# Idle products before the first load, other banks for the last down projection, and a re-ordered last normalisation in a two-layer encoder

## The chip, the cores and the metric

One core of a Trainium2 chip runs the whole program. Its engines work side by side, each on its own instruction queue: TensorE (PE; its weight loads are listed as PEld), VectorE (DVE), ScalarE (ACT), GpSimd (POOL) and SyncE (SP), which here only issues transfers. The metric is the time of one execution on the device in microseconds (us).

## The reference, cut to what matters

The reference is a two-layer encoder on 512 tokens of width 1024, all in float32. Each layer is a mixing sublayer (dilated attention, gated MLP and pooling between one input and one output projection) and a mixture of experts, each followed by a normalisation of `alpha * x + h`:

```python
def reference(x, ...):
    for l in range(DEPTH):
        h = _mixing_sublayer(x, w_in[l], w_out[l], ...)
        x = _layernorm(DEEPNORM_ALPHA * x + h, ln1_g[l], ln1_b[l])
        h = _moe(x, router_w, router_bias, w_gate[l], w_up[l], w_down[l])
        x = _layernorm(DEEPNORM_ALPHA * x + h, ln2_g[l], ln2_b[l])
    return x
```

`_moe` routes each token to two of 16 experts. An expert computes `(silu(x Wg) * (x Wu)) Wd`, with an inner width of 512; the two results are added with their gates. `_layernorm` subtracts the row's mean, divides by the root of its variance plus 1e-5, multiplies by `g` and adds `b`.

## The kernel before, in words

**Products.** Each float32 matrix is split into a high and a low part (ACT copies the high part in a rounded format, DVE subtracts it: `hilo`, L211 to L213, and for weights `emit_hi` and `emit_lo`, L184 and L192). `mm3` (L215) then issues three products per 128 x 512 block: high by high, high by low, low by high.

**Weights.** They come in blocks of 1 MB. A block is two halves; each half is split by ACT and DVE some steps ahead of its use. `half` (L203) first emits the splits up to four halves ahead (`splits_to`, L196), then hands over the half that is due. High and low parts live in a ring of four buffers each. So DVE's queue holds the splits of later halves between the other work, in the order in which the program emits them.

**The order of the work.** Every engine issues its instructions in the order of the program's text. Waits between engines follow from the data and from the reuse of buffers; a buffer or bank is free once all that touch its old content have run.

**The start.** SP fetches the activations (`xr`) and the first weights in slices. For each slice ACT and DVE make the parts, and PE starts the first projection of layer 0: four steps of 24 products, each step on one half of the weights and two slices of the activations. `load_consts` (L101) fetches constants and fills `one16`, a 128 x 128 block of 16-bit ones that the routing uses later, on POOL. The banks of PE's results come from three pools: four in `bankA`, two in `bankY`, two in `bankT`.

**An expert.** `up_piece` (L908) makes gate and up product in two `bankA` banks, `act` (L919) the activation, `turn_h` its transpose, `down_piece` (L936) the down product in two `bankY` banks, and `finish_y` (L955) scales by the gate out of the banks. Step `e` of the loop does the up product of expert `e` and the down product of expert `e - 1`. The down product goes half by half and in each half bank by bank; only for the last expert of layer 1 it goes bank by bank over all four halves, both banks in the call with `n == 0`. Experts 0 to 13 add their rows in device memory. The last two (`LAST`) are kept on the core, each as a high and a low part: `finish_y` has ACT write `y[0]` and DVE `y[1]` from each bank (L965, L966). For expert 15 these are the buffers `gl` and `y`; the pool of `y` has two buffers.

**The end of a layer.** The rows so far are fetched into four tiles `xs[0]` to `xs[3]` of 128 tokens. `add_last(i)` (L1089) forms, for each half `j` of a tile, four products on PE, which place the rows of experts 14 and 15, in a `bankT` bank, and adds the bank to `xs[i]`. What follows hangs on the tile's letter in `MODE` (L71):

- "F" and "C": DVE adds the bank (L1105); DVE takes mean and variance by the batch-norm instructions (`ln_stats`), POOL makes the factor in two small steps (L222, L223). "F" then normalises in two DVE passes over the tile (`ln_apply`, L244 and L245); "C" uses ACT and POOL too.
- "P": PE adds `xs[i]` itself by a product with the identity (L1097), ACT copies bank to tile and sums (L1103); DVE makes the mean (L1109), ACT squares the centred tile into a `y` buffer that nobody reads and sums (L1111), POOL makes the factor (L1112, L1113), and `norm` makes two DVE passes (L1128, L1129).

In layer 1 (`l + 1 == L`) `prep(i + 1)`, `norm(i)` and the store of tile `i` by SP (L1138) alternate. In layer 0 the tiles are normalised in between transposes and the first products of layer 1.

Of the kernel before, what the change touches and what calls it, by code (L numbers as in the profile page):

```python
# [59 lines left out]
def encoder(ctx, tc, a, out):  # L60
# [10 lines left out]
    MODE = ("FPCC", "FFPP")  # L71
# [29 lines left out]
    def load_consts():  # L101
        nc.sync.dma_start(cb, a["consts"])
        nc.sync.dma_start(rw, a["router_w"])
        nc.sync.dma_start(rb, a["router_b"])
        G.memset(one16, 1.0)
        G.memset(mhalf, -0.5)
# [172 lines left out]
    def layer(l, xst, xh, xl, tail):  # L279
# [656 lines left out]
        def down_piece(e, n):  # L936
            if n == 0:
                ES[e]["y"] = (bankY(), bankY())
            hh, hl = ES[e]["hT"]
            if e == NE - 1 and l + 1 == L:  # L940
                if n == 0:
                    w = [half(("e", l, e, 4 + k // 2), k % 2, NS - k) for k in range(4)]
                    for j in range(2):
                        ws = slice(j * 512, (j + 1) * 512)
                        for k in range(4):
                            mm3(ES[e]["y"][j][0:CAP], hh[:, k], hl[:, k], w[k][0][:, ws], w[k][1][:, ws], k == 0, k == 3)
# [142 lines left out]
        def add_last(i):  # L1089
            sums = None  # L1090
            if MODE[l][i] == "P":
                sums = sp.tile([128, 4], F32, name="sums", bufs=3)
            for j in range(2):
                js = slice(j * 512, (j + 1) * 512)
                b = bankT()
                if sums is not None:
                    T.matmul(b, ident, xs[i][:, js], start=True, stop=False)  # L1097
                for e in LAST:
                    lhs = ES[e]["qT"][:, i * 128:(i + 1) * 128]
                    T.matmul(b, lhs, ES[e]["yl"][0][:, js], start=sums is None and e == LAST[0], stop=False)  # L1100
                    T.matmul(b, lhs, ES[e]["yl"][1][:, js], start=False, stop=e == LAST[1])
                if sums is not None:
                    A.activation(xs[i][:, js], b, AF.Copy, accum_out=sums[:, j:j + 1])  # L1103
                else:
                    V.tensor_tensor(xs[i][:, js], xs[i][:, js], b, op=OP.add)  # L1105
# [9 lines left out]

        stats = {}
# [7 lines left out]

        def norm(i):
            if MODE[l][i] == "P":
                x, t = xs[i], stats[i][1]
                V.scalar_tensor_tensor(x, x, t[:, 2:3], gb2[0], op0=OP.add, op1=OP.mult)  # L1128
# [177 lines left out]
```

## Time and profile before

| | us |
|---|---|
| median of three runs | 1105.14 (1104.51 to 1105.29) |
| the profiled execution | 1104.96 |
| its span, from first to last instruction | 1103.3 |
| PE busy | 1055.1 |
| DVE busy | 883.8 |
| ACT busy | 740.2 |
| POOL busy | 413.7 |

The profile is of one execution. Busy times of different engines overlap. An engine's idle time matters only if the chain of work that ended last runs through it. Lengths of PE's products are modelled: products in a row overlap, and the distance of their starts tells what each takes. A number in brackets behind a row is the engine's idle time ahead of it, with the instruction that ended it.

### The profile page before, as it was taken

How to read it: one execution, taken by the hardware profiler on the slowest of the kernel's cores; microseconds unless marked ns; L12 is line 12 of the kernel's file. 1: busy time of each engine (PE TensorE's matmuls, PEld its weight loads, DVE VectorE, ACT ScalarE, POOL GpSimd, SP SyncE). 2: the span in 40 equal slices, each digit the busy share in tenths (PEclk: the TensorE clock that was granted, in tenths of full speed). 3: DMA queues.
4: the chain of work that ended last, by engine and by line, in shares of the span. 5: the costliest groups of instructions: out<-in, count | busy, mean ns of one | idle time of the engine just before them, and what ended most of it. 6: DMA issues, size and time to landing. Idle time of an engine off the chain costs nothing.

```text
span 1103.3 us, 14619 instructions
## 1 busy us (share of the span) xinstructions
PE 1055.1 (96%) x5160; PEld 817.1 (74%) x5160; DVE 883.8 (80%) x1279; ACT 740.2 (67%) x1020; POOL 413.7 (37%) x325
## 2 busy tenths in 40 slices
PE   7999999999999999999899999899899999999995
PEld 5887776777777777777578877777777777777773
DVE  4433898879999999999756249878899999999996
ACT  4334877248888888888542358862578888888872
POOL 0294554232343525230125836433224343334102
PEclk9999999999999999999899999999999999999998
DMA  8162113979999999995313422249799999999831
GB/s 292 65 229 79 68 57 128 399 272 361 351 369 357 373 350 350 361 352 178 114 45 119 150 77 77 77 154 397 280 336 369 357 354 350 364 360 366 285 122 77
DMA packets 46943, 270.90 MB, mean 246 GB/s; under 512 B 8223, under 2 KB 8479, under 8 KB 19216
## 3 DMA queue, kind: packets, MB, share of 16 engines
q1 hardware_dynamic: 37152, 246.17, 59.4%
q0 software_dynamic: 8704, 19.75, 6.8%
q10 hardware_dynamic: 1008, 3.99, 1.0%
q8 instruction: 42, 0.69, 0.2%
q14 instruction: 37, 0.30, 0.1%
HBM read 257.62 MB, written 23.46 MB: 255 GB/s over the span
## 4 chain that ended last, share of the span: by engine, by line
PE 80%; ACT 8%; DVE 8%; issue 2%; DMA 1%; POOL 0%; SPq 0%; POOLq 0%; ACTq 0%; DVEq 0%
PE bA L218 17%; PE bA L216 17%; PE bA L217 17%; PE bY L216 6%; PE bY L217 6%; PE bY L218 6%; PE bT L263 3%; ACT pr L378 2%; ACT ph L212 1%; PE bA L779 1%; DVE pl L213 1%; DVE pr L371 1%; PE bY L689 1%; DVE kl L354 1%; ACT kh L353 1%
## 5 line engine op out<-in xcount | busy, mean ns | idle before, releaser
L192 DVE TENSOR_TENSOR wlo<-raw,whi 128x1024 fp32r<-128x1024 f32 x277 | 328.8, 1224 | 93.4 <-ACT whi L184 90.5
L184 ACT ACTIVATE whi<-raw 128x1024 fp32r<-128x1024 f32 x283 | 295.7, 1060 | 102.6 <-PE bA L218 67.9
L853 POOL DMA_INDIRECT xs<-x1d,si x26 | 129.1, 4964 | 279.2 <-DVE sg L848 243.7
L216 PE MATMUL bA<-whi,gh 128*112 128x512 f32 x512 | 204.4, 399 | 3.8 <-ACT gh L212 2.7
L218 PE MATMUL bA<-whi,gl 128*112 128x512 f32 x512 | 201.7, 394 | 0.2
L217 PE MATMUL bA<-wlo,gh 128*112 128x512 f32 x512 | 200.7, 392 | 0.0
L216 PE MATMUL bA<-whi,xh 128*128 128x512 f32 x256 | 104.4, 408 | 8.3 <-ACT whi L212 7.8
L216 PEld LDWEIGHTS bA<-whi,gh 128*112 128x112 f32 x512 | 89.1, 174 | 31.4 <-ACT gh L212 3.1
L218 PEld LDWEIGHTS bA<-whi,gl 128*112 128x112 f32 x512 | 89.2, 174 | 31.0 <-DVE gl L213 1.9
L217 PEld LDWEIGHTS bA<-wlo,gh 128*112 128x112 f32 x512 | 89.1, 174 | 27.1
L218 PE MATMUL bA<-whi,xl 128*128 128x512 f32 x256 | 102.5, 400 | 0.0
L217 PE MATMUL bA<-wlo,xh 128*128 128x512 f32 x256 | 102.3, 400 | 0.0
L387 POOL TENSOR_SCALAR pr<-pr,nm 128x512 f32<-128x512 f32 x42 | 67.6, 1617 | 90.8 <-DVE nm L385 75.5
L216 PE MATMUL bY<-whi,hh 128*112 128x512 f32 x240 | 96.5, 402 | 0.0
L218 PE MATMUL bY<-whi,hl 128*112 128x512 f32 x240 | 94.5, 394 | 0.0
L217 PE MATMUL bY<-wlo,hh 128*112 128x512 f32 x240 | 94.3, 393 | 0.0
L858 POOL DMA_INDIRECT accd<-y,si x28 | 56.1, 2004 | 68.8 <-ACT y L971 61.5
L216 PEld LDWEIGHTS bA<-whi,xh 128*128 128x128 f32 x256 | 48.9, 191 | 21.2 <-ACT whi L212 8.6
L192 DVE TENSOR_TENSOR wlo<-qkt,whi 128x1024 fp32r<-128x1024 f32 x48 | 57.1, 1220 | 3.4 <-ACT whi L184 3.4
L192 DVE TENSOR_TENSOR wlo<-pr,whi 128x1024 fp32r<-128x1024 f32 x48 | 57.3, 1220 | 1.4 <-ACT whi L184 1.3
L217 PEld LDWEIGHTS bA<-wlo,xh 128*128 128x128 f32 x256 | 48.8, 191 | 12.8 <-DVE wlo L213 0.9
L218 PEld LDWEIGHTS bA<-whi,xl 128*128 128x128 f32 x256 | 48.6, 190 | 12.4 <-DVE xl L213 0.9
(249 smaller groups left out, 2085.6 us busy)
## 6 DMA issues: line engine op xcount, KB each, us to landing
raw<-w_exp SPq DMA_DIRECT2D x116, 1024.0 KB, 11.9
raw<-w_mix SPq DMA_DIRECT2D x24, 1024.0 KB, 4.8
qkt<-w_exp SPq DMA_DIRECT2D x24, 1024.0 KB, 11.6
pr<-w_exp SPq DMA_DIRECT2D x24, 1024.0 KB, 11.0
er<-w_exp SPq DMA_DIRECT2D x12, 1024.0 KB, 8.0
px<-w_exp SPq DMA_DIRECT2D x12, 1024.0 KB, 10.9
x1d<-xs POOLq DMA_DIRECT2D x8, 512.0 KB, 8.3
accd<-xs SPq DMA_DIRECT2D x8, 512.0 KB, 10.0
```

The lines of the kernel that those rows point to most:

```text
L184: A.activation(hi, raw, AF.Copy)
L192: (eng or V).tensor_tensor(lo, raw, hi, op=OP.subtract)
L212: A.activation(hi, src, AF.Copy)
L213: V.tensor_tensor(lo, src, hi, op=OP.subtract)
L216: T.matmul(ps, xh, wh, start=start, stop=False)
L217: T.matmul(ps, xh, wl, start=False, stop=False)
L218: T.matmul(ps, xl, wh, start=False, stop=stop)
L263: T.transpose(t[:, c * CAP:(c + 1) * CAP], src[0:CAP, (4 * j + c) * 128:(4 * j + c + 1) * 128], ident[0:CAP, 0:CAP])
L378: A.activation(pr[:, i, :], pr[:, i, :], AF.Exp, bias=nm[:, 0, i:i + 1], scale=-1.0, accum_out=nm[:, 1, i:i + 1])
L387: E.tensor_scalar(pr[:, i, :], pr[:, i, :], nm[:, 2, i:i + 1], None, op0=OP.mult)
L853: G.indirect_dma_start(out=dst[0:CAP], out_offset=None, in_=xd[l][:, :], in_offset=bass.IndirectOffsetOnAxis(ap=idx, axis=0), bounds_check ...
L858: G.indirect_dma_start(out=accd[l][:, :], out_offset=bass.IndirectOffsetOnAxis(ap=idx, axis=0), in_=src[0:CAP], in_offset=None, bounds_che ...
```

## The change

It has four parts. Ahead of the first transfers' use, PE gets 48 products of `one16` with itself, 128 columns each, in a `bankT` bank that nobody reads; `one16` is filled by DVE at the top of the program instead of by POOL. The down product of expert 15, in both layers, takes its two banks from `bankA`. In layer 1 its work is cut into two calls, one for each bank, in the same order. In layer 1 the letters of the tiles become "AAPP": a new mode "A", in which DVE's add also sums (no batch-norm statistics) and the mean, the square and the factor go as in "P". The end of layer 1 is written out anew: the halves of tiles 0 and 1 in turns, two in `bankT` and two in `bankY` banks; then the adds of tiles 2 and 3, with the centring passes of tiles 0 and 1 behind the first and their scaling passes and stores behind the second; then centring, scaling and store of tiles 2 and 3. For layer 0 `add_last` and `norm` do what they did.

```diff
--- before.py
+++ after.py
@@ -68,7 +68,7 @@
     NRAW, NS, NRAWX, NQ = 2, 4, 6, 4
     LEAD, VLAG, NLAG = 6, 2, 2
     LAST = (NE - 2, NE - 1)
-    MODE = ("FPCC", "FFPP")
+    MODE = ("FPCC", "AAPP")
     cp = pool(ctx, "cp")
     rawp = pool(ctx, "rawp", NRAW)
     splp = pool(ctx, "splp", NS)
@@ -102,7 +102,6 @@
         nc.sync.dma_start(cb, a["consts"])
         nc.sync.dma_start(rw, a["router_w"])
         nc.sync.dma_start(rb, a["router_b"])
-        G.memset(one16, 1.0)
         G.memset(mhalf, -0.5)
 
     xd = [dr.tile([S, D], F32, name=f"x1d{l}") for l in range(L)]
@@ -935,15 +934,16 @@
 
         def down_piece(e, n):
             if n == 0:
-                ES[e]["y"] = (bankY(), bankY())
+                bank = bankA if e == LAST[1] else bankY
+                ES[e]["y"] = (bank(), bank())
             hh, hl = ES[e]["hT"]
             if e == NE - 1 and l + 1 == L:
                 if n == 0:
-                    w = [half(("e", l, e, 4 + k // 2), k % 2, NS - k) for k in range(4)]
-                    for j in range(2):
-                        ws = slice(j * 512, (j + 1) * 512)
-                        for k in range(4):
-                            mm3(ES[e]["y"][j][0:CAP], hh[:, k], hl[:, k], w[k][0][:, ws], w[k][1][:, ws], k == 0, k == 3)
+                    ES[e]["w"] = [half(("e", l, e, 4 + k // 2), k % 2, NS - k) for k in range(4)]
+                w = ES[e]["w"]
+                ws = slice(n * 512, (n + 1) * 512)
+                for k in range(4):
+                    mm3(ES[e]["y"][n][0:CAP], hh[:, k], hl[:, k], w[k][0][:, ws], w[k][1][:, ws], k == 0, k == 3)
                 return
             for k in range(2):
                 kk = 2 * n + k
@@ -1086,23 +1086,28 @@
                         load_ln(l, "ln2", gb2)
 
 
-        def add_last(i):
-            sums = None
-            if MODE[l][i] == "P":
-                sums = sp.tile([128, 4], F32, name="sums", bufs=3)
-            for j in range(2):
-                js = slice(j * 512, (j + 1) * 512)
-                b = bankT()
-                if sums is not None:
-                    T.matmul(b, ident, xs[i][:, js], start=True, stop=False)
-                for e in LAST:
-                    lhs = ES[e]["qT"][:, i * 128:(i + 1) * 128]
-                    T.matmul(b, lhs, ES[e]["yl"][0][:, js], start=sums is None and e == LAST[0], stop=False)
-                    T.matmul(b, lhs, ES[e]["yl"][1][:, js], start=False, stop=e == LAST[1])
-                if sums is not None:
-                    A.activation(xs[i][:, js], b, AF.Copy, accum_out=sums[:, j:j + 1])
-                else:
-                    V.tensor_tensor(xs[i][:, js], xs[i][:, js], b, op=OP.add)
+        def add_half(i, j, sums, bank=bankT):
+            js = slice(j * 512, (j + 1) * 512)
+            b = bank()
+            keep = MODE[l][i] == "P"
+            if keep:
+                T.matmul(b, ident, xs[i][:, js], start=True, stop=False)
+            for e in LAST:
+                lhs = ES[e]["qT"][:, i * 128:(i + 1) * 128]
+                T.matmul(b, lhs, ES[e]["yl"][0][:, js], start=not keep and e == LAST[0], stop=False)
+                T.matmul(b, lhs, ES[e]["yl"][1][:, js], start=False, stop=e == LAST[1])
+            if keep:
+                A.activation(xs[i][:, js], b, AF.Copy, accum_out=sums[:, j:j + 1])
+            elif sums is not None:
+                V.scalar_tensor_tensor(xs[i][:, js], xs[i][:, js], 1.0, b, op0=OP.mult, op1=OP.add,
+                                       accum_out=sums[:, j:j + 1])
+            else:
+                V.tensor_tensor(xs[i][:, js], xs[i][:, js], b, op=OP.add)
+
+        def new_sums(i):
+            return sp.tile([128, 4], F32, name="sums", bufs=3) if MODE[l][i] in "PA" else None
+
+        def spread(i, sums):
             if sums is None:
                 return ln_stats(xs[i], sp, EPS2)
             t = sp.tile([128, 3], F32, name="lnt", bufs=3)
@@ -1113,6 +1118,12 @@
             G.tensor_tensor(t[:, 1:2], t[:, 0:1], mhalf[:, 0:1], op=OP.pow)
             return None, t
 
+        def add_last(i):
+            sums = new_sums(i)
+            for j in range(2):
+                add_half(i, j, sums)
+            return spread(i, sums)
+
         stats = {}
 
         def prep(i):
@@ -1122,23 +1133,50 @@
             if MODE[l][i] == "C":
                 ln_center(xs[i], stats[i])
 
+        def center(i):
+            V.scalar_tensor_tensor(xs[i], xs[i], stats[i][1][:, 2:3], gb2[0], op0=OP.add, op1=OP.mult)
+
+        def scale(i):
+            V.scalar_tensor_tensor(xs[i], xs[i], stats[i][1][:, 1:2], gb2[1], op0=OP.mult, op1=OP.add)
+
         def norm(i):
-            if MODE[l][i] == "P":
-                x, t = xs[i], stats[i][1]
-                V.scalar_tensor_tensor(x, x, t[:, 2:3], gb2[0], op0=OP.add, op1=OP.mult)
-                V.scalar_tensor_tensor(x, x, t[:, 1:2], gb2[1], op0=OP.mult, op1=OP.add)
+            if MODE[l][i] in "PA":
+                center(i)
+                scale(i)
             else:
                 ln_apply(xs[i], gb2, stats[i], MODE[l][i] == "F")
 
-        prep(0)
         if l + 1 == L:
-            for i in range(NT):
-                prep(i + 1)
-                norm(i)
+            sums = [new_sums(i) for i in range(2)]
+            for j in range(2):
+                for i in range(2):
+                    add_half(i, j, sums[i], (bankT, bankY)[j])
+            for i in range(2):
+                stats[i] = spread(i, sums[i])
+
+            def sent(i):
+                scale(i)
                 nc.sync.dma_start(out[i * 128:(i + 1) * 128, :], xs[i])
+
+            for i in range(2):
+                n = i + 2
+                sums.append(new_sums(n))
+                for j in range(2):
+                    add_half(n, j, sums[n], (bankT, bankY)[i])
+                if i == 0:
+                    center(0)
+                    center(1)
+                else:
+                    sent(0)
+                    sent(1)
+                stats[n] = spread(n, sums[n])
+            for i in range(2, NT):
+                center(i)
+                sent(i)
             ost.close()
             lst.close()
             return None
+        prep(0)
         splits_to(stream["use"] + NS)
         norm(0)
         prep(1)
@@ -1182,13 +1220,17 @@
     with ExitStack() as ist:
         ip = pool(ist, "ip", 1, side="right")
         xr = ip.tile([128, NK, S], F32, name="xr")
+        heat = bankT()
         warm = ip.tile([128, 1], F32, name="warm")
+        V.memset(one16, 1.0)
         V.memset(warm, 0.0)
         A.activation(warm, warm, AF.Copy)
 
         def first(k, n=1):
             nc.sync.dma_start(xr[:, k:k + n], a["xT"][:, k:k + n])
 
+        for _ in range(48):
+            T.matmul(heat[:, 0:128], one16, one16, start=True, stop=True)
         first(0)
         emit_load((0, 512, 1024, 2048), (lambda: first(1), lambda: first(2, 2)))
         first(4, 2)
```

## Rows read from the trace of the kernel before

**Rows 1.** The page's busy times: us, share of the span, instructions.

```profile
PE 1055.1 (96%) x5160; PEld 817.1 (74%) x5160; DVE 883.8 (80%) x1279; ACT 740.2 (67%) x1020; POOL 413.7 (37%) x325
```

**Rows 2.** The chain that ended last, by engine.

```profile
PE 80%; ACT 8%; DVE 8%; issue 2%; DMA 1%; POOL 0%; SPq 0%; POOLq 0%; ACTq 0%; DVEq 0%
```

**Rows 3.** Timeline of the start: start us, us, engine line operation [idle <-releaser].

```profile
5.46 0.80 PE L216 MATMUL bA<-whi,xh 128*128 128x512 f32 x1 [5.46 <-ACT whi L212]
...
9.79 0.79 PE L216 MATMUL bA<-whi,xh 128*128 128x512 f32 x1 [2.38 <-ACT whi L212]
...
10.52 0.79 PE L217 MATMUL bA<-wlo,xh 128*128 128x512 f32 x1
...
12.71 1.22 DVE L192 TENSOR_TENSOR wlo<-raw,whi 128x1024 fp32r<-128x1024 f32 x1
...
14.39 0.40 PE L217 MATMUL bA<-wlo,xh 128*128 128x512 f32 x1
```

**Rows 4.** Timeline of PE, layer 1's last down projection and adds.

```profile
1071.10 0.40 PE L218 MATMUL bY<-whi,hl 128*112 128x512 f32 x1
1073.36 0.48 PE L216 MATMUL bY<-whi,gh 128*112 128x512 f32 x1 [1.86 <-DVE er L966]
...
1078.77 0.40 PE L218 MATMUL bY<-whi,gh 128*112 128x512 f32 x1
...
1091.06 0.40 PE L1101 MATMUL bT<-y,q 112*128 112x512 f32 x1
```

**Rows 5.** Windows: stretch, us, busy per engine (instructions), granted clock, DMA share, GB/s.

```profile
9.79:14.10 4.31, 4.31 (x10) 3.10 (x11) 3.22 (x4) 3.17 (x3) 0.00 (x0) 1.00 1.02 408
...
529.60:533.00 3.40, 3.40 (x10) 2.42 (x10) 1.78 (x2) 1.06 (x1) 0.00 (x0) 0.50 0.00 0
...
546.70:550.10 3.40, 3.40 (x9) 2.65 (x8) 2.57 (x4) 1.18 (x4) 0.74 (x2) 0.50 0.00 0
```

**Rows 6.** Timeline of PE, layer 0's last down projection.

```profile
526.54 0.40 PE L218 MATMUL bY<-whi,hl 128*112 128x512 f32 x1
528.79 0.49 PE L216 MATMUL bY<-whi,gh 128*112 128x512 f32 x1 [1.86 <-DVE er L966]
```

**Rows 7.** Timeline of DVE, same stretch of layer 0.

```profile
528.00 1.40 DVE L966 SCALAR_TENSOR_TENSOR er<-bY,sg,er 112x512 fp32r<-112x512 f32 x2
529.32 1.21 DVE L192 TENSOR_TENSOR wlo<-raw,whi 128x1024 fp32r<-128x1024 f32 x1
...
537.06 1.40 DVE L966 SCALAR_TENSOR_TENSOR y<-bY,sg,gl 112x512 fp32r<-112x512 f32 x2
```

**Rows 8.** Timeline of DVE, end of layer 1.

```profile
1073.87 1.22 DVE L192 TENSOR_TENSOR wlo<-raw,whi 128x1024 fp32r<-128x1024 f32 x1
...
1079.92 0.75 DVE L966 SCALAR_TENSOR_TENSOR y<-bY,sg,gl 112x512 fp32r<-112x512 f32 x1 [1.98 <-ACT gl L965]
...
1096.64 1.28 DVE L1129 SCALAR_TENSOR_TENSOR xs<-xs,lnt,qkt 128x1024 f32<-128x1024 f32 x1 [0.44 <-POOL lnt L1113]
```

**Rows 9.** Timeline of PEld, 16-bit weight loads of eight small products of the routing.

```profile
238.00 0.54 PEld L841 LDWEIGHTS <-qslot 128*112 128x112 f16 x8
```

**Rows 10.** The attention's reduce: ns min/median/max, first and last start.

```profile
L371 DVE CUSTOM_DVE_ANT_0 pr<-bY,mx x64: 669/672/693, 107.3 to 725.3; 128x512 f32<-128x512 f32 x64
L371 DVE DVE_READ_ACCUMULATOR2_ANT nm<- x64: 76/83/89, 107.9 to 725.9; 128x1 f32 x64
```

**Rows 11.** Timeline of ACT, end of layer 1.

```profile
1087.91 0.60 ACT L1103 ACTIVATE xs<-bT 128x512 f32<-128x512 f32 x1 [1.10 <-PE bT L1101]
...
1092.46 1.15 ACT L1111 ACTIVATE y<-xs,lnt 128x1024 f32<-128x1024 f32 x1 [0.28 <-DVE lnt L1109]
```

**Rows 12.** Timeline of POOL, end of layer 1.

```profile
1083.48 0.24 POOL L222 TENSOR_SCALAR lnt<-lnmv 128x1 f32<-128x1 f32 x1 [26.98 <-DVE lnmv L237]
1083.80 0.58 POOL L223 TENSOR_TENSOR lnt<-lnt,mhalf 128x1 f32<-128x1 f32 x1
...
1095.13 1.47 POOL L1113 TENSOR_TENSOR lnt<-lnt,mhalf 128x1 f32<-128x1 f32 x1
```

## The prediction, made before the changed kernel was run

> **What bounds the kernel now.** The page's first part comes first: TensorE (PE) is busy 96% of the span [rows 1], and the chain that ended last gives it 80% [rows 2]. So only places where PE stands still, runs at its lower clock, or has already finished can give anything. There are three, and the change edits each. The timeline of PE with its idle times shows them.
>
> At the start PE's first product runs at 5.46 us and two more close behind; then PE idles until 9.79, when the second slice of activations and weights has come. From 10.52 to 14.39 nine products start, 3.87 / 9 = 0.43 us apart, against (1078.77 - 1073.36) / 23 = 0.235 late in the kernel [rows 3, 4]. The windows give granted clock 1.00 for 9.79 to 14.10, but 0.43 is the pace of 529.60 to 533.00, where they give 0.50 [rows 5]. I read both stretches as the lower level, 1.2 GHz, the record beginning only with a change.
>
> At the end of layer 0's experts PE stops from 526.77 (526.54 + 0.235) to 528.79 until DVE has cleared expert 14's banks, because expert 15's down product takes the same two [rows 6, 7]; right behind this, from 529.60, the granted clock is 0.50 [rows 5]. In layer 1 the same stop is 1071.33 to 1073.36, and the pace after it is 0.235: no fall [rows 4].
>
> After layer 1's last add product (1091.06) only the normalisation is left: DVE's last pass ends at 1096.64 + 1.28 = 1097.92, and just before it DVE waits for POOL [rows 4, 8].
>
> **The change, part by part.** *Idle products.* 48 products of 128 columns on ones. PE has nothing before 5.46, so they can start at about 1.2 (a small fill on DVE comes first; POOL loses its own fill). No row shows such a product. From below: a quarter of the 512 columns, 0.43 / 4 = 0.107 us at the lower level, 0.058 at the upper; eight 16-bit weight loads take 0.54, 0.07 each, and fit under the 0.107 [rows 9]. From above: load and product in line, 0.18. So 2.8 to 8.6 us; I take 0.107, PE's own pace being the nearest row: 5.1 us, ending at 6.3. The three real products behind end by 7.6; the next are not due before 9.79, which hides all of it.
>
> What it can give: with the upper level from 9.79 on, the nine steps take 9 x 0.235 = 2.1 instead of 3.87, a gain of 1.7. The next half of the weights does not take it back: its low part is ready at 12.71 + 1.22 = 13.93 [rows 3], and PE reaches it at 10.52 + 20 x 0.235 = 15.2. But the gap stays. If the clock has risen by 7.6, PE idles 2.2 us until 9.79 (more if it rises halfway, 48 x 0.058 being shorter), and the fall near 529.60 came after an idle time of 2.0. So I expect it to fall again more often than not, at some point after 9.79. Ends 0 and 1.7; I take 0.5, nearer to the row that fell.
>
> The Trainium skill (TensorE: Matmul & The Clock Gate, Part 1) says "the default state is throttled, and activity releases the throttle". By it products of ones raise the clock as real ones do, and an idle gap loses it again; the fall near 529.60 agrees with the second half, no row here shows the first.
>
> *Last down projection in other banks, layer 0.* Expert 15 takes two banks of the four-bank pool. Expert 14's up product used them one expert earlier, so they are free. PE goes on at 526.77 rather than 528.79: 2.0 us. The idle time goes, so the fall behind it should not come: eight products at 0.43 instead of 0.235, 1.6 us. The 24 products then end 3.6 earlier. What is late next is DVE: it evacuates expert 14 (528.00, two ops, 1.40), then makes the low half of this expert's last weights (529.32, 1.21) and three more halves for the next layer, all queued ahead of expert 15's evacuation [rows 7]. Without a wait for PE that is 529.4 + 4 x 1.2 = 534.2 instead of 537.06, so 2.9 come through. PE's adds, the statistics and layer 1 follow from there. From below: the stop alone, less what DVE holds back (3.6 - 2.9): 2.0 - 0.7 = 1.3. From above: the next fall, 546.70 to 550.10 at 0.50 [rows 5], goes as well, again some eight products: 2.9 + 1.6 = 4.5. I take 2.9.
>
> *The same in layer 1.* The loop there goes bank by bank, so bank 0 needs all four weight halves at once. PE could start at 1071.33, but the last half's low part is made by DVE behind expert 14's evacuation: 1073.87 + 1.22 = 1075.09 [rows 8]. The product that reads it starts at 1075.15, with one more of bank 0 and 12 of bank 1 behind: 1075.15 + 13 x 0.235 = 1078.2 instead of 1078.77. The stop of 2.0 turns into a wait for DVE; 0.55 is left. Cutting the function's work into two calls changes no order.
>
> *Summing adds and paired passes.* DVE's last op on expert 15 ends at 1079.92 + 0.75 - 0.55 = 1080.1 [rows 8]. Four adds that also sum follow, each costed as the attention's reduce with its accumulator read, 0.67 + 0.08 [rows 10]. PE feeds them 16 products from 1078.45, the last ending near 1082.4 (0.4 for its modelled length), so the fourth add ends at 1083.2. The batch-norm statistics of these tiles go; a mean and its hand-over (0.28) and a Square of 1.15 on ACT come in [rows 11], where ACT had no other work. The centring pass writes in place what Square reads, so it waits: Square until 1084.6, centre 0 until 1085.9, centre 1 until 1087.1.
>
> POOL makes each tile's factor in two steps: alone 0.24 and 0.58; the second, beside a DVE pass, 1.47, ending 0.4 after that pass (1096.60 against 1096.64 - 0.44) [rows 8, 12]. Tile 0's first step lies beside centre 0, its second beside centre 1: factor at 1087.6. Scale 0 runs to 1088.9 with tile 1's first step beside it, the second alone: 1089.6, scale 1 to 1090.9. Centre 2 to 1092.3, tile 2's factor 0.4 later, scale 2 to 1094.0, centre 3 to 1095.3, factor 1095.7, scale 3 to 1097.0. Before it was 1097.92: 0.9 gained, the 0.55 included. Each store is issued behind its scale pass as before, and the last one stays the last. From above: POOL never held up, DVE running through from 1083.5 but for Squares: about 2.4. From below: one more factor behind a whole pass, 1.28: a loss of 0.4. I take 0.9.
>
> The Trainium skill (SBUF — State Buffer, Who interferes with whom) makes this a lock: a POOL operation that reads SBUF and a DVE pass with two SBUF inputs exclude each other, and the first to start wins. By its letter a POOL step that comes first would hold DVE only for its own short length, and the sum would come nearer to 2.4; in the row of 1.47 POOL is the loser, and I go by that.
>
> **Sum.** 0.5 + 2.9 + 0.9 = 4.3 us. The profiled execution took 1104.96 (span 1103.3 and 1.66 around it), 0.18 below the median 1105.14. 1104.96 - 4.3 = 1100.66; I say 1100.7.
>
> **Rivals.** *The clock holds through the gap.* The start gives 1.7: 1104.96 - 1.7 - 2.9 - 0.9 = 1099.5. For it: the same idle of 2.0 in layer 1 brought no fall. Against: the fall near 529.60.
>
> *A buffer wait in the tail.* Square writes its unwanted squares into a two-buffer pool whose other buffer holds half of expert 15's output, read by every add product. If tile 1's Square takes that buffer, ACT stands until PE's last add, at most 1090.5 (1091.06 less 0.55); behind it in ACT's queue are four copies of 0.60 and two Squares [rows 11]: 1090.5 + 3 x 1.15 + 4 x 0.6 + 2 x 0.28 = 1096.9, then POOL's 0.8 to 1.9 and a pass of 1.28, so 1099.0 to 1100.1, and more where centre 1, held as well, pushes the passes behind it. I price it at 3 later than before: 1104.96 - 0.5 - 2.9 + 3 = 1104.6. For it: ACT works in order. Against: tile 0's buffer, which nobody reads, comes free first.
>
> *Layer 0 gives no more than layer 1* (0.6), DVE being late there in a way that I missed: 1104.96 - 0.5 - 0.6 - 0.9 = 1103.0.
>
> *Slower: the idle products overrun.* They stand in PE's queue ahead of all real work. If each waits until the one before is through, it costs what a lone product does: the first real one takes 0.80 for 512 columns [rows 3], less 384 columns at the lower pace, 0.80 - 0.32 = 0.48. They end at 1.2 + 48 x 0.48 = 24.2, and the 24th real product starts 23 x 0.235 later, at 29.6 instead of 14.39 + 10 x 0.235 = 16.7: 12.9 lost, 3.8 won, 1114.1. It begins to cost at 0.18 a product, where 1.2 + 48 x 0.18 reaches 9.79, and outweighs the 3.8 from 0.29 on. Against: loads and products overlap in this trace [rows 9].
>
> **How the numbers follow.** Forecast 0.64, clock holds 0.15, buffer wait 0.11, layer 0 like layer 1 0.06, overrun 0.04. About 0.2%, 2.2 us, is what a measurement can tell here: faster is below 1102.9. Of the forecast 0.62, all of the held clock and half of the layer-0 case are faster: 0.80. Same takes 0.02 of the forecast, 0.08 of the buffer wait and the other half of the layer-0 case: 0.13. Slower takes 0.03 of the buffer wait (with the start and layer 0 at their lower ends) and the overrun: 0.07. The forecast's own range is 1098.6 to 1102.6, from the ends of layer 0 and the tail; to hold 8 in 10 I take 1098.0 to 1103.8.
>
> **What would show it.** PE's pace after 9.79, 0.235 or 0.43, settles the first part. In layer 0 the down products should run on without idle at 0.235, and DVE's op on expert 15 should start near 3 us sooner after expert 14's last product. In layer 1 PE should stop about 1.3 us for DVE's last low half. In the tail tile 1's Square must start right behind tile 0's, and the time from the last down product to the end of the last scale pass shrink by some 0.4. A Square that waits for PE, a first real product at 10 us or later, or a layer 0 that gains under 1 us would make the forecast wrong.

## The result, and the profile after

The changed kernel took 1098.29 us (median of five, 1097.01 to 1099.34), the kernel before 1104.56 (1103.62 to 1105.29) on the same chip: a ratio of 0.9945 [0.9934, 0.9955], 6.3 us. Forecast was 1100.7, in a range of 1098.0 to 1103.8; the time lies 0.3 inside the lower end. The profiled executions are 1097.76 (span 1096.1) and 1104.96 (span 1103.3), 7.2 apart.

Four milestones split the 7.2: the 24th real product (20 behind the first one after the gap at the start), the last product of expert 14's down projection in layer 0 (c), layer 1's first product (u), and the last product of expert 14's down projection in layer 1 (g).

| stretch, us | before | after | difference |
|---|---|---|---|
| span's start to 24th real product | 16.72 | 15.80 | -0.92 |
| 24th real product to c | 509.82 | 509.80 | -0.02 |
| c to u: down projection of expert 15, adds, transposes | 23.20 | 18.60 | -4.60 |
| u to g: layer 1 | 521.36 | 520.77 | -0.59 |
| g to the end of DVE's last pass | 26.82 | 25.73 | -1.09 |

The middle of the kernel hides nothing of what is won ahead of it: the second row is 509.6 to 509.8 in all fourteen profiled executions told of here.

PE before, the 24th real product, the transposes and u:

```profile
16.72 0.39 PE L218 MATMUL bA<-whi,xl 128*128 128x512 f32 x1
...
545.57 1.09 PE L257 MATMUL bY<-cb,xs 128*128 128x128 f32 x8 [2.58 <-DVE xs L245]
...
549.74 0.57 PE L216 MATMUL bA<-whi,xh 128*128 128x512 f32 x1
```

The same after:

```profile
15.80 0.39 PE L217 MATMUL bA<-whi,xl 128*128 128x512 f32 x1
...
541.42 1.09 PE L256 MATMUL bY<-cb,xs 128*128 128x128 f32 x8 [2.59 <-DVE xs L244]
...
544.20 0.39 PE L215 MATMUL bA<-whi,xh 128*128 128x512 f32 x1
```

The page's busy time of PE and its chain, after (answering [rows 1, 2]): PE is still the bound.

```profile
PE 1053.8 (96%) x5208; PEld 818.8 (75%) x5208; DVE 880.8 (80%) x1280; ACT 742.0 (68%) x1024; POOL 415.7 (38%) x324
...
PE 80%; DVE 8%; ACT 7%; issue 2%; POOL 1%; DMA 1%; POOLq 0%; SPq 0%; ACTq 0%; DVEq 0%
```

Start, timeline of PE, after [rows 3]:

```profile
1.16 4.11 PE L1233 MATMUL bT<-one 128*128 128x128 f16 x48 [1.16 <-DVE warm L1226]
5.28 0.50 PE L215 MATMUL bA<-whi,xh 128*128 128x512 f32 x1
...
8.99 0.50 PE L215 MATMUL bA<-whi,xh 128*128 128x512 f32 x1 [2.26 <-ACT whi L211]
...
10.83 0.63 PE L217 MATMUL bA<-whi,xl 128*128 128x512 f32 x1
11.26 0.63 PE L215 MATMUL bA<-whi,xh 128*128 128x512 f32 x1
```

Windows of that stretch, after [rows 5]:

```profile
8.99:10.50 1.51, 1.28 (x4) 0.86 (x5) 0.68 (x1) 0.94 (x1) 0.00 (x0) 1.00 1.03 364
10.50:13.90 3.40, 3.40 (x10) 2.62 (x9) 2.82 (x3) 2.42 (x4) 0.00 (x0) 0.52 1.02 386
```

The 48 products of ones take 4.11 us, 0.086 each, and end at 5.27, where the first real product starts. The granted clock rises to its upper level (2.4 GHz) at 3.83, falls to the lower one (1.2 GHz) at 10.66, behind the gap, and for one stretch the products start 0.43 apart. Layer 0's last down projection, PE and then DVE, after [rows 6, 7]:

```profile
525.60 0.39 PE L217 MATMUL bY<-whi,hl 128*112 128x512 f32 x1
525.83 0.39 PE L215 MATMUL bA<-whi,gh 128*112 128x512 f32 x1
```

```profile
527.06 1.40 DVE L966 SCALAR_TENSOR_TENSOR er<-bY,sg,er 112x512 fp32r<-112x512 f32 x2
528.38 4.62 DVE L191 TENSOR_TENSOR wlo<-raw,whi 128x1024 fp32r<-128x1024 f32 x4
532.92 1.40 DVE L966 SCALAR_TENSOR_TENSOR y<-bA,sg,gl 112x512 fp32r<-112x512 f32 x2
```

PE goes on 0.23 behind expert 14's last product; DVE makes four low halves without a pause and reaches expert 15 at 532.92, 7.32 behind c instead of 10.52. PE in layer 1's last down projection, after [rows 4]:

```profile
1064.97 0.39 PE L217 MATMUL bY<-whi,hl 128*112 128x512 f32 x1
1065.20 0.39 PE L215 MATMUL bA<-whi,gh 128*112 128x512 f32 x1
...
1067.71 0.49 PE L215 MATMUL bA<-whi,gh 128*112 128x512 f32 x1 [0.27 <-ACT whi L183]
1069.01 0.48 PE L216 MATMUL bA<-wlo,gh 128*112 128x512 f32 x1 [0.81 <-DVE wlo L191]
...
1072.12 0.39 PE L217 MATMUL bA<-whi,gh 128*112 128x512 f32 x1
```

The tail on DVE, ACT and POOL, after [rows 8, 11, 12]:

```profile
1076.27 0.69 DVE L1102 SCALAR_TENSOR_TENSOR xs<-xs,bY 128x512 f32<-128x512 f32 x1 [0.24 <-PE bY L1098]
...
1078.41 2.56 DVE L1137 SCALAR_TENSOR_TENSOR xs<-xs,lnt,qkt 128x1024 f32<-128x1024 f32 x2 [1.19 <-ACT y L1116]
...
1083.45 1.29 DVE L1140 SCALAR_TENSOR_TENSOR xs<-xs,lnt,qkt 128x1024 f32<-128x1024 f32 x1 [0.72 <-POOL lnt L1118]
...
1089.42 1.28 DVE L1140 SCALAR_TENSOR_TENSOR xs<-xs,lnt,qkt 128x1024 f32<-128x1024 f32 x1 [0.44 <-POOL lnt L1118]
```

```profile
1077.13 1.15 ACT L1116 ACTIVATE y<-xs,lnt 128x1024 f32<-128x1024 f32 x1 [3.90 <-DVE lnt L1114]
...
1078.41 1.16 ACT L1116 ACTIVATE y<-xs,lnt 128x1024 f32<-128x1024 f32 x1
```

```profile
1078.47 1.28 POOL L1117 TENSOR_SCALAR lnt<-sums 128x1 f32<-128x1 f32 x1 [28.08 <-ACT y L1116]
...
1087.91 1.47 POOL L1118 TENSOR_TENSOR lnt<-lnt,mhalf 128x1 f32<-128x1 f32 x1
```

Tile 1's Square starts right behind tile 0's (1078.41). From PE's last down product to the end of the last pass it is 1089.42 + 1.28 - 1072.12 = 18.58; before, 1096.64 + 1.28 - 1078.77 = 19.15.

### The profile page after: what moved, and what is told of

Same layout as the page of the kernel before. It is cut to its first block, busy times and chain, and to the rows that moved or that the text cites. A ratio compares the mean times of both kernels' runs of the same rounds, so it can differ in the third digit from the quotient of the medians.

```text
span 1096.1 us, 14724 instructions
## 1 busy us (share of the span) xinstructions
PE 1053.8 (96%) x5208; PEld 818.8 (75%) x5208; DVE 880.8 (80%) x1280; ACT 742.0 (68%) x1024; POOL 415.7 (38%) x324
## 4 chain that ended last, share of the span: by engine, by line
PE 80%; DVE 8%; ACT 7%; issue 2%; POOL 1%; DMA 1%; POOLq 0%; SPq 0%; ACTq 0%; DVEq 0%
PE bA L217 18%; PE bA L215 18%; PE bA L216 17%; PE bY L215 6%; PE bY L217 6%; PE bY L216 6%; PE bT L262 3%; PE bA L778 1%; ACT pr L377 1%; ACT ph L211 1%; DVE pl L212 1%; DVE pr L370 1%; PE bY L688 1%; DVE kl L353 1%; DVE qs L354 1%
## 5 line engine op out<-in xcount | busy, mean ns | idle before, releaser
L215 PE MATMUL bA<-whi,gh 128*112 128x512 f32 x528 | 210.6, 399 | 3.9 <-ACT gh L211 2.7
L216 PE MATMUL bA<-wlo,gh 128*112 128x512 f32 x528 | 207.1, 392 | 0.8 <-DVE wlo L191 0.8
L215 PEld LDWEIGHTS bA<-whi,gh 128*112 128x112 f32 x528 | 91.9, 174 | 32.7 <-ACT gh L211 3.1
L216 PEld LDWEIGHTS bA<-wlo,gh 128*112 128x112 f32 x528 | 92.1, 174 | 28.8 <-DVE wlo L191 1.1
```

What stands on the lines that cost most here:

```text
L215: T.matmul(ps, xh, wh, start=start, stop=False)
L216: T.matmul(ps, xh, wl, start=False, stop=False)
```

## The experiments

Kernels are compared with the kernel before on the same chip; a ratio stands with its 95% interval, and kernels timed on different chips are compared by their ratios. Milestones are of the one profiled execution of each.

### Parts of the change, each alone on the kernel before

**heat_only**: the idle products.

```diff
-        G.memset(one16, 1.0)
...
+        heat = bankT()
...
+        V.memset(one16, 1.0)
...
+        for _ in range(48):
+            T.matmul(heat[:, 0:128], one16, one16, start=True, stop=True)
```

> The kernel before with the 48 idle products alone. Theory 1 (the gap loses the clock again): the clock rises while they run and falls again soon after the second slice's products begin, so PE's pace from 10.5 us on is 0.43 for most of the next 3 us; 0 to 0.5 us are won. Theory 2 (the held clock is worth its full 1.7): 1.5 to 1.9 us won. Theory 3 (the 0.9 us by which the changed kernel led from 15 us on comes from the loads and not from the clock): PE's first product behind the gap starts near 9.0 instead of 9.8 only by chance of a run, and the start differs from run to run by as much; then this kernel may begin behind the gap at 9.8.

Measured: 1103.65, ratio 0.9996 [0.9987, 1.0006]. The gap was 2.40, the clock fell at 10.74, and the 20 products behind the gap took 6.81 instead of 6.93. Alone, the part can't be told from nothing.

**banks_layer0** and **banks_layer1**: other banks in one layer.

```diff
-                ES[e]["y"] = (bankY(), bankY())
+                bank = bankA if e == LAST[1] and l == 0 else bankY      # banks_layer0
+                bank = bankA if e == LAST[1] and l + 1 == L else bankY  # banks_layer1
+                ES[e]["y"] = (bank(), bank())
```

> The kernel before with expert 15's down product in the four-bank pool in layer 0 alone. Theory 1 (stop and clock): the 24 down products run on without a stop at 0.235, DVE's op on expert 15 starts about 3.2 us sooner after expert 14's last product, and 3.2 us are won in all runs, up to 4.6 where the second fall (behind the transposes) stays away as it did in the changed kernel. Theory 2 (the second fall is lost to the change for good): 4.6 us won in every run. Theory 3 (the 4.5 us of the changed kernel's layer 0 hang on the other edits): under 2 us won.

> The kernel before with expert 15's down product in the four-bank pool in layer 1 only. Theory 1: the stop of 2.0 us behind expert 14's last product becomes a wait of about 1 us for DVE's last low half; the last of the 24 products lies 7.15 us behind expert 14's last one instead of 7.67 (0.5 gained), or instead of 9.25 where the old stop also cost the granted clock (2.1 gained; the profiles of heat_only and l0_hold showed 9.25, those of before, banks_layer0 and tail_only 7.67). The tail behind it keeps its 19.15. Median 0.5 to 1.3 us below the kernel before, about 0.9. Rival: the place is worth the 0.5 alone, the clock never matters: 0.5 or less. Second rival: worth nothing, the tail's first reader (DVE) is late anyway: same time as before.

Measured: 1100.71, ratio 0.9970 [0.9958, 0.9981], for layer 0, and 1102.77, 0.9986 [0.9977, 0.9995], for layer 1. In layer 0 DVE reaches expert 15 at 7.31 behind c, as in the full change. In layer 1 the last down product lies 7.15 behind g, against 7.67 or 7.68 in three of the five profiled executions with the old banks there, and 9.25 and 9.23 in two (heat_only, l0_hold). Those two show why, here heat_only's stop and the window behind it:

```profile
1071.28 0.48 PE L215 MATMUL bY<-whi,gh 128*112 128x512 f32 x1 [1.86 <-DVE er L965]
```

```profile
1072.28:1075.69 3.41, 3.41 (x9) 2.42 (x8) 0.74 (x1) 0.00 (x0) 0.00 (x0) 0.50 0.00 0
```

The granted clock is at the lower level there too. The stop in layer 1 costs the clock in some executions; the one that I had read was not one of them [rows 4]. The stop in layer 0 cost it in all four profiled executions that have it with nothing in it (before, heat_only, tail_only, banks_layer1), where DVE reaches expert 15 at 10.51 to 10.53 behind c.

**tail_only**: the summing adds and the paired passes, with the old banks and no idle products.

```diff
-    MODE = ("FPCC", "FFPP")
+    MODE = ("FPCC", "AAPP")
...
-            for i in range(NT):
-                prep(i + 1)
-                norm(i)
+            sums = [new_sums(i) for i in range(2)]
...
```

> The kernel before with the new end of layer 1 alone (modes, order, banks of the adds), no idle products and expert 15 in its old banks. Theory 1: 0.4 to 0.6 us won, as the changed kernel's time from the last down product to the end of the last scaling pass shrank from 19.15 to 18.58. Theory 2 (the swap of banks in layer 1 does all of it, the new order nothing): 0.0. In a single run's profile the last pass should end 18.6 us after the last down product.

Measured: 1102.94, ratio 0.9988 [0.9979, 0.9997]. Last down product to end 18.58, as in the full change. The four ratios multiplied give 0.9940, the full change 0.9945: within the intervals, some 0.001 to either side of each part, the parts add up.

### The two causes in layer 0

**l0_hold**: the kernel before, with products of ones in the stop, into a bank that nobody reads. The stop stays; the clock should not fall.

```diff
+            if e == LAST[1] and l == 0:
+                hb = bankA()
+                for _ in range(30):
+                    T.matmul(hb[:, 0:128], one16, one16, start=True, stop=True)
             if e == LAST[1]:
                 ES[e - 1]["qT"] = PO["ep"].tile([CAP, S], F32R, name="hh", bufs=1)
```

> The kernel before with 30 idle products placed in layer 0's stop between the down products of experts 14 and 15; the stop itself stays. Theory 1 (the stop also costs the clock): the fall behind the stop goes, the eight products at 0.43 run at 0.235, and 1.0 to 1.6 us are won though no work is removed. Theory 2 (the stop costs only its 2.0 us of waiting, the clock's fall there is chance): no change, within 0.5. If the 30 products outlast the stop (over 2.0 us), the down product starts later by the rest.

PE, its window and then DVE behind c (526.24):

```profile
526.48 1.85 PE L1082 MATMUL bA<-one 128*128 128x128 f16 x30
528.50 0.49 PE L216 MATMUL bY<-whi,gh 128*112 128x512 f32 x1 [0.17 <-DVE er L966]
```

```profile
526.40:534.00 7.60, 7.43 (x56) 5.81 (x55) 6.29 (x7) 5.66 (x8) 0.00 (x0) 1.00 0.02 4
```

```profile
535.22 1.40 DVE L966 SCALAR_TENSOR_TENSOR y<-bY,sg,gl 112x512 fp32r<-112x512 f32 x2
```

The stop is as long as before (2.26 from c to the next down product, before 2.25), the clock stays at its upper level, and DVE reaches expert 15 at 535.22 - 526.24 = 8.98 behind c: of the 3.2 between 10.52 and 7.32, 1.54 is the clock and 1.66 the stop. The whole kernel took 1104.14, ratio 0.9994 [0.9985, 1.0003], a gain of 0.7 us whose interval of -0.3 to 1.7 holds both theories: the time alone does not tell them apart, the profile does. In the profiled execution the 20 products of the start took 7.55 instead of 6.93, and the clock fell in layer 1's stop, which cost 9.23 - 7.67 = 1.56; with that the gain is gone from this execution.

### The start, from both sides

**no_heat**: the full change without the idle products. **gap_fill**: the full change with 36 more of them in the gap.

```diff
-        for _ in range(48):                                   # no_heat
-            T.matmul(heat[:, 0:128], one16, one16, start=True, stop=True)
...
+            if k and h == 0 and i == 0 and heats:             # gap_fill, in front of slice 2's first product
+                for _ in range(36):
+                    T.matmul(heats[0][:, 0:128], one16, one16, start=True, stop=True)
+                heats.clear()
```

> The changed kernel without the 48 idle products. Theory 1 (they win almost nothing, as the clock falls in the gap behind them): 0 to 0.4 us slower than the changed kernel (1098.3), the 24th real product 6.6 to 7.6 us after the first one behind the gap, against 6.81 with them. Theory 2 (they are worth 0.9 or more): 1099.2 or later. If their fixed rhythm also moves the later falls of the clock, the falls at layer 0's transposes should come back; under theory 1 those are chance with or without them.

> The changed kernel with 36 more idle products in the gap, behind the first three real ones. Theory 1 (the gap lets the clock fall): the clock stays at the upper level from its rise before 7 us on, the 24th real product starts about 5.3 us after the first one behind the gap instead of 6.8, and 1.5 us are won, 1096.8. Theory 2 (the fall comes from something else, such as idle products not counting as work): it falls again near 10.7, nothing is won. Theory 3 (they are in the way): they last beyond the second slice's coming and lose up to 1 us.

Measured: 1098.87, ratio 0.9951 [0.9937, 0.9964], without; 1097.43, 0.9941 [0.9927, 0.9955], with the gap filled. By the ratios the 48 products are worth 0.7 us (0 to 0.4 expected), and the filling 0 to 0.4 more (1.5 expected; the changed kernel has 0.9945, and 0.9941 when run once more as after_again, below). The order is as expected, but the intervals reach over 1 us to either side and overlap: the times decide nothing here. The milestones are clear: the 20 products behind the gap take 6.72 without idle products and 5.26 with the gap filled. Two kernels with the 48 alone show that the length of the gap does not decide by itself. The stretch behind the gap in early_low (below), PE and window:

```profile
8.54 0.50 PE L215 MATMUL bA<-whi,xh 128*128 128x512 f32 x1 [1.95 <-ACT whi L211]
```

```profile
8.54:13.80 5.26, 5.03 (x20) 3.87 (x21) 3.13 (x4) 3.18 (x3) 0.00 (x0) 1.00 1.01 377
```

and in the changed kernel run once more (after_again):

```profile
8.84 0.75 PE L215 MATMUL bA<-whi,xh 128*128 128x512 f32 x1 [1.89 <-ACT whi L211]
```

```profile
8.92:12.33 3.41, 3.41 (x8) 2.34 (x9) 2.40 (x3) 2.11 (x2) 0.00 (x0) 0.50 1.01 387
```

An idle of 1.95 kept the clock, one of 1.89 lost it. Of five profiled executions with the 48 alone, three lost it (20 products in 6.53 to 6.81) and two kept it (5.26, 5.27); those two were the ones where the second slice came first, at 8.03 and 8.54 (the others 8.84 to 9.24); five executions make that a hint and no rule. That arrival is a matter of the execution: 8.0 to 9.8 over all kernels, with no order by kernel.

> The changed kernel once more, on the same chip as the two combined ones: 1098 to 1099 us by its earlier median of 1098.3, 0.9945 of the kernel before. Its profile shows which of the things that vary from execution to execution come back: second slice of inputs at 8 to 9.8 us, a fall of the granted clock behind the transposes of layer 0 (1.4 us) or none, one in the start's gap.

Measured: 1098.61, ratio 0.9941 [0.9927, 0.9954].

gap_fill's profiled execution was the longest of its five, 1101.18 (the others 1097.24 to 1097.48). PE in layer 1 shows where it lost:

```profile
596.72 2.80 PE L490 MATMUL bT<-v,sm 128*128 128x256 f32 x8 [2.04 <-DVE v L483]
```

A wait of 2.04 for DVE that is 0.35 at most in the other thirteen traces, and the clock fell behind it, at 597.77: u to g is 524.90 instead of 520.77. The trace shows what made DVE late: a weight half that landed late. ACT's split of it starts 37.06 behind u, in the changed kernel 34.53; DVE's low half follows it, and behind that in DVE's queue the work up to the awaited result:

```profile
580.42 1.06 ACT L183 ACTIVATE whi<-raw 128x1024 fp32r<-128x1024 f32 x1 [6.46 <-DMA raw<-w_mix]
```

The 2.53 between them reach PE as the 2.04. No edit touches that load; why it landed late stays open.

### The waits left in the tail

**early_low**: the last low half in layer 1 made ahead of expert 14's evacuation. **one_step**: the first of the two steps of a tile's factor on DVE, both steps issued in front of the tile's centring pass.

```diff
                 down_piece(e - 1, 1)
+                if e == LAST[1] and l + 1 == L:               # early_low
+                    splits_to(stream["use"] + NS)
                 finish_y(e - 1)
...
-            G.tensor_scalar(t[:, 0:1], sums[:, 2:3], 1.0 / D, EPS2, op0=OP.mult, op1=OP.add)
...
+            def factor(E):                                    # one_step, E = V in layer 1
+                E.tensor_scalar(t[:, 0:1], sums[:, 2:3], 1.0 / D, EPS2, op0=OP.mult, op1=OP.add)
...
         def center(i):
+            if l + 1 == L:
+                stats[i][0](V)
```

> The changed kernel with the last weight half of expert 15 in layer 1 split ahead of expert 14's evacuation, both on ACT and DVE. Theory 1 (in layer 1 the stop became a wait for DVE's queue): PE's waits of 0.27 and 0.81 go, expert 15's last product starts 5.6 us after expert 14's instead of 7.15, minus what a wait for the high part keeps, and 1.0 to 1.5 us are won: 1097.0. Theory 2 (PE would then wait for expert 14's evacuation elsewhere, at the first adds): under 0.3.

> The changed kernel with the first of the two factor steps moved from POOL to DVE in layer 1's end, ahead of the centring pass. Theory 1 (each POOL step is held up behind a DVE pass, so that half the steps mean half the waits): the time from the last down product to the last pass's end shrinks from 18.58 to about 17.2, DVE's waits for POOL of 0.36, 0.72, 0.44 and 0.44 shrink to 0.4 in all at most, 1.2 to 1.6 us won. Theory 2 (DVE's own queue is what takes the time): less than 0.4, or a loss by the four added small operations (0.2 each, 0.5).

Measured: early_low 1096.46, ratio 0.9933 [0.9919, 0.9946]; one_step 1096.70, 0.9935 [0.9921, 0.9948]. By the ratios they are 0.9 to 1.3 and 0.7 to 1.1 us below the changed kernel, with intervals that overlap its own.

In early_low the wait for the low half is gone, and the last down product lies 5.91 behind g instead of 7.15 (5.6 expected): 1.24 by the profile. The end lies 24.17 behind g instead of 25.73; the other 0.32 come from the tail, where one of POOL's steps was not held up, DVE and then POOL:

```profile
1084.53 1.31 DVE L1142 SCALAR_TENSOR_TENSOR xs<-xs,lnt,qkt 128x1024 f32<-128x1024 f32 x1 [0.44 <-POOL lnt L1120]
...
1087.14 1.28 DVE L1142 SCALAR_TENSOR_TENSOR xs<-xs,lnt,qkt 128x1024 f32<-128x1024 f32 x1
```

```profile
1084.58 0.19 POOL L1119 TENSOR_SCALAR lnt<-sums 128x1 f32<-128x1 f32 x1
```

The step starts 0.05 behind a pass like the held ones, but takes 0.19 instead of 1.28, and the last pass no longer waits for POOL. The edit of early_low does not reach there, so this is chance.

In one_step the last product to the end is 18.18 instead of 18.58, where 17.2 was expected. DVE still waits for POOL's second step, 0.88 in all (0.4 expected), and a wait of 0.58 for ACT's copy of the last tile has come in:

```profile
1083.01 0.21 DVE L1114 TENSOR_SCALAR lnt<-sums 128x1 f32<-128x1 f32 x1 [0.58 <-ACT xs L1100]
...
1087.89 1.28 DVE L1146 SCALAR_TENSOR_TENSOR xs<-xs,lnt,qkt 128x1024 f32<-128x1024 f32 x1 [0.44 <-POOL lnt L1119]
```

Beyond these 0.40 its profiled execution won at the start, where the second slice came at 8.03 and the clock held.

### All together

**combo_nofill**: the full change with gap_fill, early_low and one_step. **combo**: the same, with 30 products of ones where PE waits for DVE ahead of layer 0's transposes.

```diff
         norm(0)
         prep(1)
+        hb = bankY()
+        for _ in range(30):
+            T.matmul(hb[:, 0:128], one16, one16, start=True, stop=True)
         ost.close()
```

> The changed kernel with three of the additions tried alone: idle products in the start's gap, the last low half made ahead of expert 14's evacuation in layer 1, and the factor's first step on DVE in the last normalisation. Theory 1 (only what the milestones of the profiles show adds up): 1.5 from the held clock at the start, 1.4 from the early low half, 0.4 from the factor: 3.3 less than the changed kernel, about 1095.0. Theory 2 (the medians of the single tries add up): 0.9 + 1.8 + 1.6 = 4.3 less, about 1094.0. Theory 3 (the single tries gained by the same thing, a clock held at the start): 1.5 to 1.9 less in all, about 1096.6. In the profile: 24 products behind the start's gap in 5.3, last down product 5.9 behind expert 14's, 17.9 from it to the end.

> The same with 30 idle products behind the transposes of layer 0 as well, where PE waits and the granted clock fell afterwards in some of the profiled executions (7 to 8 products at the lower pace, 1.4 us between the transposes and layer 1's first product: 4.2 to 4.4 instead of 2.8). Theory 1: the fall does not come any more; 2.8 in the profile, and the median 0.3 to 1.4 less than without, depending on how often it came. Rival: the idle products stand in front of the real ones and add what they take at most, 30 x 0.06 = 1.8 us, so slower by 0 to 1.8 than without them.

Measured: 1096.45 (1095.48 to 1097.31), ratio 0.9927 [0.9913, 0.994], and 1094.24 (1093.98 to 1094.34), ratio 0.9908 [0.9893, 0.9923]. after_again, on the same chip, lies at 1096.25 to 1099.09: combo is 4.4 us faster, and the ranges don't meet. Against combo_nofill it is 2.2 faster, more than the 0.3 to 1.4 expected; part of that lies outside the program's span, which is 1.9 shorter (median 1092.55 against 1094.4), since combo_nofill's runs take 1.85 to 2.56 us around the span and combo's 1.64 to 1.71. PE and the window behind the transposes, without the 30 products:

```profile
539.87 1.64 PE L256 MATMUL bY<-cb,xs 128*128 128x128 f32 x8 [2.60 <-DVE xs L244]
```

```profile
539.87:543.40 3.53, 3.53 (x13) 3.10 (x14) 1.74 (x4) 2.21 (x4) 0.74 (x2) 0.55 0.30 128
```

and with them:

```profile
536.74 1.85 PE L1199 MATMUL bY<-one 128*128 128x128 f16 x30
539.49 1.09 PE L256 MATMUL bY<-cb,xs 128*128 128x128 f32 x8 [0.90 <-DVE xs L244]
```

```profile
539.49:542.90 3.41, 3.41 (x19) 2.98 (x20) 1.62 (x4) 2.21 (x4) 0.74 (x2) 1.00 0.34 137
```

From the transposes to layer 1's first product it is 4.38 without and 2.78 with the products, and they cost nothing: their bank is free, PE would have stood still, and the transposes start 15.81 behind c in both. combo_nofill's time is that of the third theory, its milestones are those of the first (5.26, 5.88, 18.20); its u to g is 521.31, 0.5 to 0.9 more than in the two executions of the changed kernel, and 0.35 of it is the wait for DVE seen in gap_fill, behind the same load. combo's granted clock stays at the upper level from 6.89 to the tail. At its start the products of ones overran the gap, at a cost of some 0.1:

```profile
1.17 5.30 PE L1251 MATMUL bT<-one 128*128 128x128 f16 x48 [1.17 <-DVE warm L1244]
...
7.32 2.18 PE L280 MATMUL bT<-one 128*128 128x128 f16 x36
9.31 0.48 PE L215 MATMUL bA<-whi,xh 128*128 128x512 f32 x1
```

ACT's high part of the second slice was ready at 8.69, 0.62 ahead of the product at 9.31, but the 20 products behind that took 4.75 instead of 5.26, as they no longer waited for the low part.

## Why the prediction was right, and where its sizes were off

**The idle products** (0.5, ends 0 and 1.7). The mechanism stands: the products are hidden in the gap, and the clock rose at 3.83 and fell behind the gap. Their 0.086 us is a mean over both levels; in combo, where the clock rose at 6.89 only, the 48 took 5.30, 0.110 each, against 0.107 forecast. The size of the gain can't be told from nothing: heat_only gives 0.4 us, the full change against no_heat (0.9951 - 0.9945) x 1104 = 0.7, and the intervals of both take in nothing. The profiled pair shows 0.92 at the start, but 0.80 of it is the second slice, which came at 8.99 instead of 9.79; the 20 products themselves went from 6.93 to 6.81. The rival of the held clock came true in two of five executions. What it rested on, that an idle time of one length may or may not bring a fall, was right.

**Layer 0** (2.9, ends 1.3 and 4.5). Right in place, cause and size. PE's 2.0 and the clock's 1.6 came through DVE's queue as 3.2 (l0_hold splits it into 1.66 and 1.54); four low halves back to back took 4.62, forecast 4 x 1.2. banks_layer0 measures 3.3 [2.1, 4.6]. The upper end named the second fall. Its absence is what made the profiled pair 4.60: transposes to layer 1's first product took 4.2 before and 2.8 after. The executions do not show that to be the change's doing: after_again has the fall. Of the profiled executions with a wait of 2.6 ahead of the transposes, five of seven with the new banks in layer 0 have it, and four of five with the old ones. In no_heat the clock fell earlier, at 534.78 among the adds, behind a wait of 1.32; the wait ahead of the transposes was then 0.96, and c to u 18.59 as in the changed kernel. A fall ahead of a wait for another engine cost nothing there.

**Layer 1's banks** (0.55). The position is right, 7.67 to 7.15 = 0.52, with 0.27 + 0.81 of waits where I had put some 1.3. Here is the mis-sized term: "the pace after it is 0.235: no fall" was read from one execution and priced as if it held in all. banks_layer1 measures 1.5 us [0.6, 2.5]. Two of five profiled executions with the old banks fell there and lost 1.57, which makes 0.52 + 0.4 x 1.57 = 1.15 on average, within that interval.

**The tail** (0.9 less 0.55 = 0.35). Measured 19.15 - 18.58 = 0.57. The chain I wrote out held step by step: measured from the last down product, the fourth add ends at 4.8 (forecast 5.0), the second centring pass at 8.9 (8.9), the end at 18.6 (18.8). The buffer wait did not come: tile 1's Square follows tile 0's at once. POOL's steps beside a pass took 1.28 to 1.59, and DVE waited for POOL four times, 1.96 in all; those waits are what was left to win there.

The Trainium skill (SBUF — State Buffer, Who interferes with whom) lets the first to start win between a POOL operation that reads SBUF and a DVE pass with two SBUF inputs. The changed kernel's rows agree: each POOL step stretched to 1.28 or more starts behind a pass of DVE's (1078.47 behind 1078.41, 1087.91 behind 1087.70), and the passes keep their 1.28. The case by which that rule would have brought the gain nearer to 2.4 came once in six profiled executions with both steps on POOL, in early_low, and brought 0.32; by its start that step too was behind the pass, so the starts in the profile do not tell who wins.

**The sum.** 4.3 forecast, 6.3 measured, of the profiled pair 7.2; and the median of the kernel before, 1104.56, lies 0.4 below the execution that the forecast subtracts from. By the parts timed alone: start 0.4, layer 0 3.3, layer 1 1.5, tail 1.3 [0.3, 2.3], together 6.5. Against the forecast's terms that is some 0.95 more each in layer 1 and in the tail, and 0.4 more in layer 0. Layer 1's is the clock, as above; the tail's own 1.3 is more than the 0.57 of its profile, and how much of that is chance its interval can't say. That the time stayed inside the range is in part luck: the range got its width from the ends of layer 0 and the tail, and nothing in it stood for the clock in layer 1. The 0.59 of the pair in layer 1 (u to g) stays unexplained: 0.2 of it are shorter waits of PE, and the stretch is 520.45 to 521.36 over the executions without gap_fill's long wait.

## What to carry to other kernels

A short stop of TensorE can cost twice, its own length and the clock behind it in a part of the executions: price it at its length plus the chance of a fall (four of four behind layer 0's stop, two of five behind layer 1's), even where the one profile at hand shows none. Products of ones in a wait that stays cost nothing here where a bank was free and they ended before the wait did, and no fall came behind a wait that held them. combo, with them in both places, has four times within 0.4 us of each other; combo_nofill, without those ahead of the transposes, five within 1.8, the changed kernel on the same chip five within 2.8.

## What was not expected of the hardware

The rise of the granted clock behind the first products came at 3.82 to 6.89 us in the eight executions with 48 idle products, and at 12.54 to 14.63 in the six without, with the same instructions ahead of it. The same idle time of 1.86 in layer 1's stop kept the clock in the kernel before [rows 4] and lost it in heat_only, and the 2.59 ahead of the transposes kept it in the changed kernel and lost it in after_again: the length of a stop alone does not decide. The Trainium skill (TensorE: Matmul & The Clock Gate, Part 1) says that the same kernel meets the change at another product from run to run; the traces agree, and show that the same holds for the fall.
